# Hybrid decoder block: fewer expert pairs scattered, down projections moved behind the next gate and up, the router's end written out in order

## The chip, the cores and the metric

One core of a Trainium2 chip runs the whole program. The metric is the device time of one execution in microseconds. The kernel before took 1235.06 us (median of 3 runs, 1234.50 to 1239.01). Engines are called as in the profile: PE does matmuls (PEld loads its weights), DVE is the vector engine, ACT the scalar engine, POOL is GpSimd, SP only issues DMAs here. Sixteen DMA engines serve all queues.

## The reference

The block works on one sequence of 512 tokens with 1024 channels, all in float32. It has two parallel branches (a state-space scan and latent attention), a cross-attention to 256 memory rows, and a mixture of experts. The change touches the end of the cross-attention and the mixture, which is:

```
t = rms_norm(h, norm_moe)
g_logits = t @ w_rg + b_rg              # 4 groups
e_logits = t @ w_re + b_re              # 32 experts, 8 in each group
g_sel = argmax(g_logits);  g_w = softmax(g_logits)[g_sel]
top_v, top_i = top_k(e_logits of group g_sel, 2)
w_top = softmax(top_v) * g_w
h += sum over the 2 chosen experts e of
     w_top[e] * ((silu(t @ w_gate[e]) * (t @ w_up[e])) @ w_down[e])
return rms_norm(h, norm_final)
```

Each expert has gate and up weights of 1024 x 256 and down weights of 256 x 1024, 3 MB in float32, and 32 of them are read.

## The kernel before, in words

Everything up to the router has its order of instructions chosen by a planner, which works with a cost model of its own; from `chain` on (line 1111) the order on every engine and queue is the written one.

**Low parts.** Matmuls of the first stages split each weight into a high part (tile `WH`) and a low part. The low parts go in turn through three places: one in tile `WLa`, two in `WLb` (lines 134 to 152). When the stages are over, `YB` takes the place of `WLa`, and the one-hot matrices `OHt` take that of `WLb` (lines 1074 to 1076).

**Router.** `tok_proj` (line 857) adds the output of the cross-attention to `h`, 512 channels (`c`) and 128 tokens (`t`) at a time, and calls `router_tile(c, t)` for each. That squares `h` for the norm, transposes it on PE, copies the transposes to `tT` on ACT, and multiplies them by the router's weights (`logits`, 4 float32 matmuls of 36 columns, two instructions each). `keep_warm(n)` issues n transposes whose result nobody reads. Then DVE works through the routing in some 40 small steps: norm, logits, top group, top two experts, the place of each token within its expert (`ppos`, on PE), and `sl`, the slot number of each token's two choices.

**Slots.** Each expert has 64 slots, and a pair of experts `pr` 128 rows. Tokens past 64 in one expert go to a loop at the very end, which runs as often as needed. A one-hot matrix (tokens by slots) multiplied by token numbers and weights gives each slot's token: `onehots` builds it on DVE, 256 slots (a piece `c`, two pairs) at a time, and `places` reads out tokens, weights and scatter addresses with 8 matmuls and some 16 DVE steps of two or 16 columns. For pairs 0 and 1 `first_rows` reads only the token numbers, so that their gathers can start.

**A pair.** `fetch` or `first_rows` lets POOL gather the 128 rows of `h` from their copy `tD` in memory. `dispatch` transposes them (8 transposes) and scales them on DVE into `XG`. `gate_up` multiplies with both experts' weights, each on its 64 columns of the array (32 instructions), then asks SP for gate and up weights of pair `pr + 3`, whose tiles it has just freed. `hidden` makes silu(gate) * up on ACT and DVE, `turn` transposes that. `down` multiplies with the down weights (16 instructions). SP asks for the down weights of pair `pr + 3` behind `down_rows(pr)`; it has three places for them as well.

**Back to the tokens.** For pairs below `NS` = 11, `down_rows` weighs the result on ACT into `YB`, and POOL scatters the rows into a table `yD` in memory (one half for the first choice, one for the second). For the others `weigh` makes a high and a low part in `WHe` (ACT, then DVE), `ones_at` builds the one-hot matrix `oT` on DVE, and `combine` multiplies the two (16 matmuls, 8 DVE adds into `h`). The scattered rows come back as 16 table pieces `Yt` of 128 x 512 (lines 1387 to 1400): `left_rows` asks for two on POOL's queue, `add_left` adds two to `h` on DVE and asks for the next two. In pairs 12 to 15 that happens twice a pair: before `dispatch`, and behind `combine`.

**The loop** (lines 1405 to 1446) runs, for each pair: `gate_up`, `hidden`, from pair 12 on `add_left`, `dispatch` of the next pair, `places` or `onehots`, `fetch`, `down_rows` of the pair before, `turn`, and from pair 12 on `combine` of the pair before and `add_left`. Behind it `down_rows` and `combine` of pair 15 and the final norm follow, with the output in four DMAs.

Of the kernel before, what the change touches and what calls it, by code (L numbers as in the profile page):

```python
# [29 lines left out]
def block(tc, nc, I, out, dbg=None):  # L30
# [101 lines left out]
        return w  # L132

    WH = sb.tile([128, 3, 1024], F32R, name="WHt", tag="WH")
    WLa = sb.tile([128, 1, 1024], F32R, name="WLta", tag="WLa")
    WLb = sb.tile([128, 2, 1024], F32R, name="WLtb", tag="WLb")
    WL = (WLa[:, 0], WLb[:, 0], WLb[:, 1])
    nsp = [0]

    def wsplit(shape):  # L140
# [895 lines left out]
    def router_tile(c, t):  # L1036

        if t == 0:
            tT[c] = sb.tile([128, 4, S], F32, name=f"tT{c}", tag="wr", bufs=2)
            if not c:  # L1040
                plg.append(pB("plg"))
        jk = tmp([128, 512], BF, name="jk2")
        A.activation(jk, h[:, t, c * 512:(c + 1) * 512], AF.Square, scale=1.0 / 32, accum_out=sq2[:, c, t:t + 1])
        p = pB("ptt")
        for d in range(4):
            T.transpose(p[:, d * 128:(d + 1) * 128], h[:, t, c * 512 + d * 128:c * 512 + (d + 1) * 128], ident)
        o, v = tT[c][:, :, t * 128:(t + 1) * 128], p.rearrange("p (d t) -> p d t", d=4)
        A.activation(o, v, AF.Copy)
        if c:
            nc.scalar.dma_start(tD[t * 128:(t + 1) * 128], h[:, t])  # L1050
        if t > 1:
            logits(c, t - 2)
        if t == NT - 1:
            logits(c, t - 1)
            logits(c, t)
    tok_proj(I["w_xo"][0], tk(oxh, oxl), 1.0, router_tile, pB)
    keep_warm(45)
    if dbg:
        dbg("h2", h)
    rt = sb.tile([128, 512], F32, name="rt", tag="acT")  # L1060
# [10 lines left out]
    GRt = sb.tile([128, 3, D], F32, name="GRt", tag="WH")  # L1071
    GR = [GRt[:, i] for i in range(2)]
    XG = GRt[:, 2].rearrange("p (k n) -> p k n", k=KD)
    YB = sb.tile([128, D], F32, name="YB", tag="WLa")
    OHt = sb.tile([128, 2, NT, 256], F32R, name="OHt", tag="WLb")
    OHs = [OHt[:, i] for i in range(2)]
    NG4 = NT * 4
    gl, el = T4(rtile(NG4)), rtile(NT * 32)
    g1, jk1, jk2 = rtile(NT), rtile(NT), rtile(NG4)
# [19 lines left out]
        yield V.tensor_tensor(oh, rv, bcn(jk, n), op=OP.is_equal)  # L1099

    HG, HT, PI, W2 = {}, {}, {}, []
    def onehots(c, js=(0, 1), ts=range(NT)):

        n = slice(js[0] * 128, js[-1] * 128 + 128)
        s_ = slc[:, c - 1] if c else sl
        for t in ts:
            a = rt2[:, 256:512][:, n]
            V.tensor_scalar(a, iot1[:, n], s_[:, 0, t:t + 1], None, op0=OP.is_equal)
            stt(OHs[c % 2][:, t, n], iot1[:, n], s_[:, 1, t:t + 1], a, OP.is_equal, OP.add)

    chain = ExitStack()
    chain.enter_context(tc.manual_schedule())
# [34 lines left out]
    for s in range(2):  # L1147
        V.tensor_tensor(big2[:, s], EE[:, s], qs_, op=OP.mult)
    V.reduce_sum(sl, big2, axis=AX.X)
    onehots(0, (0,))  # L1150
    V.tensor_copy(qs_, pe_)
    V.tensor_tensor(slc.rearrange("p c s t -> p c (s t)"), sl.rearrange("p s t -> p (s t)")[:, None, :].to_broadcast([128, 7, 8]),
                    c256[:, :, None].to_broadcast([128, 7, 8]), op=OP.add)
# [86 lines left out]
    def places(c):  # L1240

        p = pA("pinf")
        for j in range(2):
            for t in range(NT):
                T.matmul(p[:, j * 8:j * 8 + 8], OHs[c % 2][:, t, j * 128:(j + 1) * 128], info[:, t],
                         start=t == 0, stop=t == NT - 1)
        pi = PI[c] = ov[:, 216 + c % 3 * 26:242 + c % 3 * 26]
        V.tensor_copy(pi[:, :16], p[:, :16])
        col = lambda i: pi[:, :16].rearrange("p (j x) -> p x j", x=8)[:, i]
        ix, sx = (ov[:, o + c % 3 * 2:o + 2 + c % 3 * 2].bitcast(I32) for o in (300, 306))  # L1250
        u, wa, w, hr, r = (pi[:, 16 + 2 * i:18 + 2 * i] for i in range(5))
# [64 lines left out]

    def weigh(p, n, hf, w):

        WHe, = W2
        yh, yl = (WHe[:n, i, hf * 512:(hf + 1) * 512] for i in range(2))  # L1320
        A.activation(yh, p[:n], AF.Copy, scale=w)
        stt(yl, p[:n], w, f(yh), OP.mult, OP.subtract)

    def combine(oT, n, after=None):

        WHe, = W2
        for t, hf in ((0, 0), (1, 0), (0, 1), (1, 1), (2, 0), (3, 0), (2, 1), (3, 1)):
            hs = slice(hf * 512, (hf + 1) * 512)
            p = pA("pcm")
            T.matmul(p, oT[:n, t * 128:(t + 1) * 128], WHe[:n, 0, hs], start=True, stop=False)  # L1330
            T.matmul(p, oT[:n, t * 128:(t + 1) * 128], WHe[:n, 1, hs], start=False, stop=True)
            V.tensor_add(h[:, t, hs], h[:, t, hs], p)
            if after and hf:
                after(t)
# [23 lines left out]
            nc.sync.dma_start(outr[:, t], fo[:, t])  # L1358

    first_rows(0)  # L1360
    onehots(0, (1,))
    first_rows(1)
    gfin = fo = None
    wcol = lambda pr: PI[pr // 2][:, 20 + pr % 2:21 + pr % 2]
    hcol_ = lambda pr: PI[pr // 2][:, 22 + pr % 2:23 + pr % 2]
    tcol = lambda pr: PI[pr // 2][:, pr % 2 * 8:pr % 2 * 8 + 1]

    def down_rows(pr):

        if pr >= NS:  # L1370
            for hf in range(2):
                weigh(down(pr, hf), 128, hf, wcol(pr))
        else:
            for hf in range(2):
                A.activation(YB[:, hf * 512:(hf + 1) * 512], down(pr, hf), AF.Copy, scale=wcol(pr))  # L1375
            sx = ov[:, 306 + pr // 2 % 3 * 2 + pr % 2:307 + pr // 2 % 3 * 2 + pr % 2].bitcast(I32)
            G.indirect_dma_start(out=yD, out_offset=bass.IndirectOffsetOnAxis(ap=sx, axis=0), in_=YB, in_offset=None,
                                 bounds_check=2 * S - 1, oob_is_err=False)
        if pr + 3 < NP:
            load_down(pr + 3)  # L1380

    def add_rows(pr, after=None):
        combine(ones_at(128, tcol(pr)), 128, after)

    Yt, ny = [], [0, 0]

# [12 lines left out]
            ny[1] += 1  # L1399
        left_rows(n)  # L1400

    keep_warm(22)
    dispatch(0)
    keep_warm(8)
    for pr in range(NP):
# [12 lines left out]
            continue  # L1418
        if pr == 1:
            turn(0)  # L1420
        if pr > NS:
            add_left(2)
        if pr + 1 < NP:
            dispatch(pr + 1)
        c = pr // 2 + 2
        if pr % 2 and c < NP // 2:
            places(c)
        elif c < NP // 2:
            onehots(c)
        if pr + 3 < NP:  # L1430
            fetch(pr + 3)
        down_rows(pr - 1)
        if pr == NS:
            Yt.append(sb.tile([128, 2, 512], F32, name="Yt", tag="WLa"))
            left_rows(2)
            W2.append(sb.tile([128, 2, D], F32R, name="WHe", tag="WLb"))
        turn(pr)
        if pr == 2:
            overflow()
        if pr > NS:  # L1440
            add_rows(pr - 1)
            add_left(2)
        if pr == NP - 2:
            fo = gslot(NP - 3, 0, [128, NT, D], "fo")
            gfin = gslot(NP - 3, 1, [128, D], "gfin")
# [105 lines left out]
```

## Time and profile before

| | us |
|---|---|
| median of 3 runs | 1235.06 |
| the profiled execution | 1232.03 |
| its span | 1229.9 |
| PE busy | 1157.7 (94%) |
| DVE busy | 709.1 (58%) |
| ACT busy | 497.2 (40%) |
| POOL busy | 98.8 (8%) |
| granted PE clock, mean | 0.976 |

All times in the rows below are microseconds from the span's start. Busy times are those of one execution; an engine that is busy is not one that sets the end. A line number is that of the kernel before, and where a helper issues the instruction, that of the helper: most three-operand DVE steps stand at line 55, and all warm-up transposes at line 77. A matmul's duration includes its way through the array, so durations of neighbours overlap. A granted clock of 1.00 is 2.4 GHz, of 0.50 is 1.2 GHz.

### The profile page before, as it was taken

The numbers are of one execution on the slowest core, as the hardware profiler recorded it, in microseconds if no ns is written. First come the engines' busy times: TensorE is split into PE (matmuls) and PEld (weight loads), VectorE is DVE, ScalarE is ACT, GpSimd is POOL, SyncE is SP. The second block draws the span as 40 slices with busy tenths as digits, with TensorE's granted clock in tenths as the row PEclk, the third lists the DMA queues.
The fourth block names the chain that finished last, engine by engine and source line by source line (L and its number), as shares of the span: only waits on it lengthen the run. The fifth ranks groups of instructions, "written<-read, shape, count | busy, mean of one in ns | idle before, by whom it ended". The sixth has DMA issues, their size and how long they took to land. (4 is left out here: it accounts for less than half of the span.)

```text
span 1229.9 us, 15623 instructions
## 1 busy us (share of the span) xinstructions
PE 1157.7 (94%) x5893; PEld 846.8 (69%) x5893; DVE 709.1 (58%) x1456; ACT 497.2 (40%) x941; POOL 98.8 (8%) x122
## 2 busy tenths in 40 slices
PE   8999999999999999999999999999998999786981
PEld 6787777777888888887777889888886343333441
DVE  4387878778762335547775738636326644223564
ACT  5445765866542223557774325535320111011012
POOL 0101102121000000101110000000000211011111
PEclk9999999999999999999999999999998999888996
DMA  3542432432322323311124364643725999999921
GB/s 113 157 120 62 146 94 95 133 110 69 103 88 83 103 88 128 88 46 50 56 86 172 121 221 131 196 159 123 288 85 227 410 420 419 419 419 420 413 111 70
DMA packets 104331, 210.43 MB, mean 171 GB/s; under 512 B 13624, under 2 KB 71765, under 8 KB 91966
## 3 DMA queue, kind: packets, MB, share of 16 engines
q1 hardware_dynamic: 96782, 193.11, 43.6%
q0 software_dynamic: 6896, 14.20, 3.5%
q10 hardware_dynamic: 576, 2.10, 0.4%
q8 instruction: 47, 0.77, 0.3%
q14 instruction: 30, 0.25, 0.1%
HBM read 199.33 MB, written 14.22 MB: 174 GB/s over the span
## 5 line engine op out<-in xcount | busy, mean ns | idle before, releaser
L151 ACT ACTIVATE WHt<-wr 128x1024 fp32r<-128x1024 f32 x125 | 132.2, 1059 | 266.5 <-PE pa L126 157.3
L152 DVE TENSOR_TENSOR WLtb<-wr,WHt 128x1024 fp32r<-128x1024 f32 x82 | 100.0, 1221 | 109.1 <-ACT WHt L151 56.8
L1287 PE MATMUL pgu<-gu,GRt 128*64 128x512 f32 x512 | 122.2, 617 | 11.1 <-DMA gu<-in_w_exp_up_dram 11.1
L126 PE MATMUL pa<-uh,WHt 128*128 128x512 f32 x488 | 128.0, 399 | 2.7 <-ACT WHt L151 2.7
L126 PE MATMUL pa<-ul,WHt 128*128 128x512 f32 x488 | 124.8, 393 | 0.0
L126 PEld LDWEIGHTS pa<-uh,WHt 128*128 128x128 f32 x488 | 89.8, 188 | 23.4 <-ACT WHt L151 3.1
L126 PEld LDWEIGHTS pa<-ul,WHt 128*128 128x128 f32 x488 | 90.5, 188 | 18.9 <-issue 0.7
L1287 PEld LDWEIGHTS pgu<-gu,GRt 128*64 128x64 f32 x512 | 39.6, 142 | 82.7 <-issue 77.5
L152 DVE TENSOR_TENSOR WLta<-wr,WHt 128x1024 fp32r<-128x1024 f32 x42 | 53.5, 1274 | 65.2 <-ACT WHt L151 41.4
L126 PE MATMUL pa<-uh,WLtb 128*128 128x512 f32 x320 | 82.6, 395 | 0.0
L55 DVE SCALAR_TENSOR_TENSOR ea<-ea,pgu 128x256 f32<-128x256 f32 x16 | 6.7, 420 | 110.6 <-ACT ea L1276 110.5
L1276 ACT ACTIVATE ea<-pgu,ov 128x256 f32<-128x256 f32 x16 | 7.6, 474 | 155.3 <-PE pgu L1287 144.1
L126 PEld LDWEIGHTS pa<-uh,WLtb 128*128 128x128 f32 x320 | 59.2, 188 | 13.0 <-issue 1.2
L713 DVE TENSOR_REDUCE sm<-psc 128x1 f32<-128x512 f32 (+2 forms) x64 | 30.4, 489 | 23.5 <-PE psc L711 20.3
L126 PE MATMUL pa<-uh,WLta 128*128 128x512 f32 x168 | 42.3, 391 | 0.0
L1307 PE MATMUL py<-dn,aT 128*64 128x512 f32 x176 | 40.2, 598 | 0.0
L1219 POOL DMA_INDIRECT GRt<-tD,ov x16 | 16.2, 1010 | 272.9 <-DMA dw<-in_w_exp_down_dram 144.9
L714 ACT ACTIVATE Pq<-psc,sm 128x512 f32<-128x512 f32 (+2 forms) x64 | 33.2, 528 | 10.6 <-DVE sm L713 10.1
L1330 PE MATMUL pcm<-WHe,oT 128*128 128x512 f32 x40 | 18.8, 470 | 18.8 <-DVE oT L1314 18.8
L126 PEld LDWEIGHTS pa<-uh,WLta 128*128 128x128 f32 x168 | 31.3, 188 | 6.4
L55 DVE SCALAR_TENSOR_TENSOR y<-pa,cols,y 128x509 f32<-128x509 f32 (+2 forms) x48 | 34.7, 743 | 1.6 <-ACT y L385 1.4
L1375 ACT ACTIVATE YB<-py,ov 128x512 f32<-128x512 f32 x22 | 15.1, 687 | 45.7 <-PE py L1307 42.7
(528 smaller groups left out, 2351.4 us busy)
## 6 DMA issues: line engine op xcount, KB each, us to landing
gu<-in_w_exp_gate_dram SPq DMA_DIRECT2D x32, 1024.0 KB, 20.8
gu<-in_w_exp_up_dram SPq DMA_DIRECT2D x32, 1024.0 KB, 21.4
wr<-in_w_in_dram SPq DMA_DIRECT2D x26, 1024.0 KB, 5.4
dn<-in_w_exp_down_dram SPq DMA_DIRECT2D x22, 1024.0 KB, 22.5
dw<-in_w_exp_down_dram SPq DMA_DIRECT2D x10, 1024.0 KB, 21.7
wr<-in_w_ssd_out_dram SPq DMA_DIRECT2D x8, 1024.0 KB, 4.9
wr<-in_w_xkv_dram SPq DMA_DIRECT2D x8, 1024.0 KB, 5.0
S6t<-ac_d SPq DMA_DIRECT2D x24, 256.0 KB, 4.2
```

The lines of the kernel that those rows point to most:

```text
L55: V.scalar_tensor_tensor(o, a, s, b, op0=op0, op1=op1, **k)
L126: T.matmul(o, a(k)[x], b(k)[y], start=first and n == 0, stop=last and n == 3 * nk - 1)
L151: A.activation(h, raw, AF.Copy)
L152: lo.tensor_tensor(l, raw, f(h), op=OP.subtract)
L713: V.reduce_max(mx, dst, axis=AX.X, negate=True)
L714: A.activation(P[:, ROFF[qc]:ROFF[qc] + n], dst, AF.Exp, bias=mx, accum_out=sm[:, 1, s, qc:qc + 1])
L1219: G.indirect_dma_start(out=GR[pr % 2], out_offset=None, in_=tD, in_offset=bass.IndirectOffsetOnAxis(ap=ix, axis=0), **k)
L1276: A.activation(a[:, :256], p[:n, :256], AF.Tanh, scale=hr)
L1287: T.matmul(p[s * 64:(s + 1) * 64].rearrange("p (j n) -> p j n", j=2), XG[:, k, s * 64:(s + 1) * 64], gu[s][:, :, k], start=k == 0, stop=k ...
L1307: T.matmul(p[s * 64:(s + 1) * 64], aT[:, k, s * 64:(s + 1) * 64], dn[s][:, k, hf * 512:(hf + 1) * 512], start=k == 0, stop=k == 1)
L1330: T.matmul(p, oT[:n, t * 128:(t + 1) * 128], WHe[:n, 0, hs], start=True, stop=False)
L1375: A.activation(YB[:, hf * 512:(hf + 1) * 512], down(pr, hf), AF.Copy, scale=wcol(pr))
```

## The change

- `WLa` and `WLb` become three tiles `WL0`, `WL1`, `WL2`. `YB` takes the place of the first, the two one-hot matrices that of the others. Piece 1 alone has its one-hots in the second, all other pieces in the first.
- `NS` goes from 11 to 7: pairs 7 to 15 go through `weigh` and `combine`. Their weighted rows stand in tiles that `rt` and `rt2` leave free, and in `WL2`.
- From pair 8 on `down_rows` of the pair before follows `gate_up` and `hidden` directly, ahead of `dispatch`. In it `oT` is built first, and kept for `combine`.
- Table pieces: the first two are asked at pair 7, and `add_left` stands once in each of pairs 8 to 15, behind `combine`. `onehots` stands behind that.
- From `router_tile(1, 0)` on PE runs in the written order. `logits` stands before or behind the transposes of the last tiles as the diff shows, and `keep_warm` has 34 transposes instead of 45, all behind the last logits.
- The one-hots of pairs 0 and 1 are built by three DVE operations over all four token tiles each, instead of eight over one tile each.
- `keep_warm` ahead of the first `dispatch` has 6 transposes instead of 22.

```
-    WLa = sb.tile([128, 1, 1024], F32R, name="WLta", tag="WLa")
-    WLb = sb.tile([128, 2, 1024], F32R, name="WLtb", tag="WLb")
-    WL = (WLa[:, 0], WLb[:, 0], WLb[:, 1])
+    WL = [sb.tile([128, 1024], F32R, name=f"WLt{i}", tag=f"WL{i}") for i in range(3)]
...
-    NP, NS = 16, 11
+    NP, NS = 16, 7
...
             if not c:
                 plg.append(pB("plg"))
+            else:
+                ending.enter_context(tc.manual_schedule(engines={mybir.EngineType.PE}))
+        if t == NT - 1:
+            logits(c, t - 2)
...
-        if t > 1:
+        if t == NT - 2:
             logits(c, t - 2)
         if t == NT - 1:
             logits(c, t - 1)
             logits(c, t)
+    ending = ExitStack()
     tok_proj(I["w_xo"][0], tk(oxh, oxl), 1.0, router_tile, pB)
-    keep_warm(45)
+    keep_warm(34)
+    ending.close()
...
+    def onehots(c):
+        for t in range(NT):
+            o = OHs[c == 1][:, t]
+            V.tensor_scalar(o, iot1[:, :256], slc[:, c - 1, 0, t:t + 1], None, op0=OP.is_equal)
+            stt(o, iot1[:, :256], slc[:, c - 1, 1, t:t + 1], f(o), OP.is_equal, OP.add)
+
+    def first_onehots(j):
+        it = iot1[:, None, j * 128:(j + 1) * 128].to_broadcast([128, NT, 128])
+        o2 = [tmp([128, 512], name="oa").rearrange("p (t n) -> p t n", t=NT) for _ in range(2)]
+        for s in range(2):
+            V.tensor_tensor(o2[s], it, bcn(sl[:, s], 128), op=OP.is_equal)
+        V.tensor_tensor(OHs[0][:, :, j * 128:(j + 1) * 128], o2[0], o2[1], op=OP.add)
...
         if pr >= NS:
+            oTs[pr] = ones_at(128, tcol(pr))
             for hf in range(2):
                 weigh(down(pr, hf), 128, hf, wcol(pr))
...
     def add_rows(pr, after=None):
-        combine(ones_at(128, tcol(pr)), 128, after)
+        combine(oTs.pop(pr), 128, after)
...
-    keep_warm(22)
+    keep_warm(6)
     dispatch(0)
...
-        if pr > NS:
-            add_left(2)
+        late = pr > NS
+        if late:
+            down_rows(pr - 1)
         if pr + 1 < NP:
             dispatch(pr + 1)
         c = pr // 2 + 2
         if pr % 2 and c < NP // 2:
             places(c)
-        elif c < NP // 2:
+        elif c < NP // 2 and not late:
             onehots(c)
         if pr + 3 < NP:
             fetch(pr + 3)
-        down_rows(pr - 1)
-        if pr == NS:
-            Yt.append(sb.tile([128, 2, 512], F32, name="Yt", tag="WLa"))
-            left_rows(2)
-            W2.append(sb.tile([128, 2, D], F32R, name="WHe", tag="WLb"))
+        if not late:
+            down_rows(pr - 1)
         turn(pr)
         if pr == 2:
             overflow()
-        if pr > NS:
+        if late:
             add_rows(pr - 1)
             add_left(2)
+            if pr % 2 == 0 and c < NP // 2:
+                onehots(c)
+        if pr == NS:
+            Yt.append(sb.tile([128, 2, 512], F32, name="Yt", tag="WL0"))
+            left_rows(2)
+            W2.append([sb.tile([128, 512], F32R, name=f"Wx{i}", tag=t) for i, t in enumerate(("acT", "selP"))])
+            W2.append([x[:, i * 512:(i + 1) * 512] for x in [sb.tile([128, 1024], F32R, name="Wy", tag="WL2")] for i in range(2)])
```

## Rows read from the trace of the kernel before

**Rows 1.** Busy time by stretch: stretch, length, each engine, PE clock, DMA share, GB/s.
```profile
930.00:960.00 30.00, 27.52 (x147) 18.41 (x147) 21.28 (x94) 0.89 (x3) 3.99 (x4) 0.84 0.57 221
...
1080.00:1110.00 30.00, 25.64 (x111) 11.50 (x112) 7.15 (x16) 3.37 (x7) 3.05 (x3) 0.89 1.01 419
...
1170.00:1200.00 30.00, 25.31 (x108) 12.00 (x106) 19.97 (x34) 4.46 (x8) 3.22 (x6) 0.94 0.26 96
```

**Rows 2.** Timeline, router's end, all engines: start, duration, instruction, [idle before <- releaser].
```profile
918.84 0.60 ACT L1048 ACTIVATE tT<-ptt 128x512 f32<-128x512 f32 x1 [0.52 <-PE ptt L1046]
...
920.73 2.38 PE L77 MATMUL pw<-ident 128*128 128x128 f32 x20
...
922.95 0.98 PE L1033 MATMUL plg<-MI,tT 128*128 128x36 f32 x8
...
923.97 0.31 DVE L1122 TENSOR_TENSOR rt<-plg,MI 128x144 f32<-128x144 f32 x1 [3.48 <-PE plg L1033]
...
931.04 0.29 DVE L1108 TENSOR_SCALAR rt<-MI 128x128 f32<-128x128 f32 x1
...
933.49 0.35 DVE L55 SCALAR_TENSOR_TENSOR OHt<-MI,rt 128x128 fp32r<-128x128 f32 x1
...
935.22 1.02 POOL L1219 DMA_INDIRECT GRt<-tD,ov  x1 [144.89 <-DMA dw<-in_w_exp_down_dram]
...
937.36 4.96 PE L77 MATMUL pw<-ident 128*128 128x128 f32 x22
```

**Rows 3.** The gathers of line 1219: from issue to landing.
```profile
DMA to landing us min/median/max: 4.8/8.3/9.7
```

**Rows 4.** Timeline of SP's queue: the last gate and up piece.
```profile
1143.75 0.33 SPq L977 DMA_DIRECT2D gu<-in_w_exp_up_dram  x1
```

**Rows 5.** The gate and up loads of line 977: from issue to landing.
```profile
DMA to landing us min/median/max: 6.9/21.4/24.3
```

**Rows 6.** DMA issues: table pieces, KB each, median us to landing.
```profile
Yt<-yD POOLq DMA_DIRECT2D x16, 256.0 KB, 6.5
```

**Rows 7.** Busy time by pair: pair 12, then pair 13.
```profile
1113.43:1142.06 28.63, 18.83 (x75) 9.58 (x74) 9.59 (x16) 2.89 (x6) 4.30 (x6) 0.82 1.02 418
1142.06:1160.36 18.30, 16.08 (x75) 7.26 (x75) 10.70 (x19) 2.12 (x4) 2.17 (x4) 1.00 1.01 414
```

**Rows 8.** Busy time while `places` runs: its matmuls, then its DVE steps.
```profile
1075.06:1076.10 1.04, 1.04 (x13) 1.02 (x13) 1.00 (x3) 0.00 (x0) 0.00 (x0) 1.00 1.04 433
1076.80:1079.50 2.70, 2.70 (x14) 0.72 (x10) 2.30 (x17) 0.69 (x1) 1.01 (x1) 1.00 1.01 422
```

**Rows 9.** Timeline of PE, expert pairs.
```profile
944.42 7.09 PE L1287 MATMUL pgu<-gu,GRt 128*64 128x512 f32 x32
...
1044.02 1.07 PE L1287 MATMUL pgu<-gu,GRt 128*64 128x512 f32 x2
1047.09 7.08 PE L1287 MATMUL pgu<-gu,GRt 128*64 128x512 f32 x30 [2.00 <-DMA gu<-in_w_exp_up_dram]
...
1065.00 9.22 PE L1287 MATMUL pgu<-gu,GRt 128*64 128x512 f32 x30 [4.79 <-DMA gu<-in_w_exp_up_dram]
...
1135.76 0.76 PE L1330 MATMUL pcm<-WHe,oT 128*128 128x512 f32 x1 [9.80 <-DVE oT L1314]
...
1156.41 0.47 PE L1330 MATMUL pcm<-WHe,oT 128*128 128x512 f32 x1 [2.22 <-DVE oT L1314]
...
1180.78 7.09 PE L1287 MATMUL pgu<-gu,GRt 128*64 128x512 f32 x32
...
1193.37 0.47 PE L1330 MATMUL pcm<-WHe,oT 128*128 128x512 f32 x1 [1.69 <-DVE oT L1314]
...
1203.01 0.47 PE L1330 MATMUL pcm<-WHe,oT 128*128 128x512 f32 x1 [2.06 <-DVE oT L1314]
```

**Rows 10.** Timeline of DVE: a table piece added in pair 12, combine's adds in pair 13.
```profile
1130.10 0.69 DVE L1398 TENSOR_TENSOR h<-h,Yt 128x512 f32<-128x512 f32 x1 [7.57 <-DMA Yt<-yD]
...
1157.15 4.87 DVE L1332 TENSOR_TENSOR h<-h,pcm 128x512 f32<-128x512 f32 x8 [0.89 <-PE pcm L1331]
```

More of the change, by code (lines that the diff above doesn't have):

```diff
@@ L1073, in block @@
     XG = GRt[:, 2].rearrange("p (k n) -> p k n", k=KD)
-    YB = sb.tile([128, D], F32, name="YB", tag="WLa")
-    OHt = sb.tile([128, 2, NT, 256], F32R, name="OHt", tag="WLb")
-    OHs = [OHt[:, i] for i in range(2)]
+    YB = sb.tile([128, D], F32, name="YB", tag="WL0")
+    OHs = [sb.tile([128, NT, 256], F32R, name=f"OH{i}", tag=f"WL{i + 1}") for i in range(2)]
     NG4 = NT * 4
@@ L1101, in block @@
     HG, HT, PI, W2 = {}, {}, {}, []
[L1102 to L1109, printed above, removed]
+    def onehots(c):
[9 more added lines that the diff above has]
+        V.tensor_tensor(OHs[0][:, :, j * 128:(j + 1) * 128], o2[0], o2[1], op=OP.add)
     chain = ExitStack()
@@ L1149, in block @@
     V.reduce_sum(sl, big2, axis=AX.X)
-    onehots(0, (0,))
+    first_onehots(0)
     V.tensor_copy(qs_, pe_)
@@ L1244, in places @@
             for t in range(NT):
-                T.matmul(p[:, j * 8:j * 8 + 8], OHs[c % 2][:, t, j * 128:(j + 1) * 128], info[:, t],
+                T.matmul(p[:, j * 8:j * 8 + 8], OHs[c == 1][:, t, j * 128:(j + 1) * 128], info[:, t],
                          start=t == 0, stop=t == NT - 1)
@@ L1317, in weigh @@
     def weigh(p, n, hf, w):
-        WHe, = W2
-        yh, yl = (WHe[:n, i, hf * 512:(hf + 1) * 512] for i in range(2))
+        yh, yl = (x[:n] for x in W2[hf])
         A.activation(yh, p[:n], AF.Copy, scale=w)
@@ L1324, in combine @@
     def combine(oT, n, after=None):
-        WHe, = W2
         for t, hf in ((0, 0), (1, 0), (0, 1), (1, 1), (2, 0), (3, 0), (2, 1), (3, 1)):
@@ L1329, in combine @@
             p = pA("pcm")
-            T.matmul(p, oT[:n, t * 128:(t + 1) * 128], WHe[:n, 0, hs], start=True, stop=False)
-            T.matmul(p, oT[:n, t * 128:(t + 1) * 128], WHe[:n, 1, hs], start=False, stop=True)
+            T.matmul(p, oT[:n, t * 128:(t + 1) * 128], W2[hf][0][:n], start=True, stop=False)
+            T.matmul(p, oT[:n, t * 128:(t + 1) * 128], W2[hf][1][:n], start=False, stop=True)
             V.tensor_add(h[:, t, hs], h[:, t, hs], p)
@@ L1360, in block @@
     first_rows(0)
-    onehots(0, (1,))
+    first_onehots(1)
     first_rows(1)
@@ L1366, in block @@
     tcol = lambda pr: PI[pr // 2][:, pr % 2 * 8:pr % 2 * 8 + 1]
+    oTs = {}
     def down_rows(pr):
         if pr >= NS:
+            oTs[pr] = ones_at(128, tcol(pr))
             for hf in range(2):
```

## The prediction

> **What bounds the kernel now.** I read the busy time by stretch first. Where the experts run, the 16 DMA engines are busy 1.01 of the time from pair 3 on, and they drop to 0.26 in the last full stretch [rows 1]. So the experts are bound by their weights until about 1170 us, and by what the engines still have to do after that. Then I read the timelines at both ends of that stream. Ahead of it stands the router: its last logits, a chain of small DVE steps, the first gather, and gate and up of pair 0. Only when that last one ends are pair 3's weights asked, so each us won there moves the whole stream. Behind it, gate and up of pair 15 start at 1180.78 [rows 9], some 15 us after their last piece can have landed: it was asked at 1143.75 and the median landing is 21.4 us, which gives 1165.2 [rows 4, 5]. So from pair 12 on PE lags behind the weights. Pair 12 took 28.63 us with 18.83 busy, pair 13 took 18.30 with 16.08 busy [rows 7]. The reason is seen in pair 12: DVE stood 7.57 us for a piece of the table [rows 10], and PE 9.80 us behind it, for the one-hot matrix `oT` [rows 9].
>
> Sums below are made against the profiled execution: span 1229.9 us, time 1232.03, which lies 3.0 below the median of 1235.06. The 3.0 is added back at the end.
>
> **Router's end.** Before, 20 warm-up transposes (2.38 us) run ahead of the last logits, which so start at 922.95, though their input was there at 919.44 (the ACT copy from 918.84, 0.60 us); DVE takes the logits up at 923.97 [rows 2]. Written out, the order has half a logits group more (0.5 us) ahead of the last transposes, so the copy behind them ends at 919.95; then follow the last group's 0.98 and some 0.3 of handing over. DVE starts at about 921.2: 2.8 us won. The bounds are 0 (other engines are still placed by the planner) and 3.5 (no wait at all behind the copy). The rn steps on DVE, which must be done too, end at 920.5 and hide. The 34 transposes left (0.119 us each, 4.0 us) end at 925.3, before the one-hot of the router is there, so they hold nobody up.
>
> **First one-hots.** Eight small DVE operations run from 931.04 to 933.84, 2.80 us [rows 2]. In their place come three of 128x512 with two tensors. The nearest row is the add of a table piece, 0.69 us [rows 10]: 2.0 us. The four matmuls behind them no longer run beside them, +0.4. Net 0.4 won, between -0.5 and +1.0. The gather, issued at 935.22 before [rows 2], is issued at about 932.0.
>
> **Gather and first pair.** A gather lands 4.8 to 9.7 us after its issue, median 8.3 [rows 3]. The first has the 4.8 of a queue running empty. Issued earlier, it falls among the weights of pair 2, so I take 6.5: landed at 938.5. Before, 22 transposes (937.36, 4.96 us) end just before 942 and dispatch follows, 2.5 us ahead of gate and up at 944.42 [rows 2, 9]. With 6 of them dispatch waits for the gather instead, from 938.5: gate and up at 941.0, 3.4 won. Against it stands the clock. Those 22 transposes take 0.225 us each and the 20 before took 0.119 [rows 2], so PE ran at 1.2 GHz here, and the granted clock over 930 to 960 is 0.84 [rows 1]. With less work ahead of it, gate and up of pair 0 can begin at 1.2 GHz. A gate and up that did after a wait took 9.22 us for 30 instructions, where 7.08 is the rule [rows 9]: 2.1 lost at that, I take 1.1. So the stream starts G = 2.3 us earlier, bounds -3.6 (all of pair 0 at half rate) and 4.5 (landing in 4.8, no clock lost).
>
> The Trainium skill (DMA: Bandwidth & Descriptors, section "Issuing engines are not separate DMA queues") says that DMAs from whatever engine run on the same 16 engines and interleave. By that alone the early gather would take the loaded 8.3 us and G would be 0.5, the sum 1219. The trace agrees in so far as that 8.3 is the median over all 16 gathers, most of them issued into the running stream [rows 3].
>
> **The stream.** Four scatters less: each moves at most 128 rows of 4 KB, half of them filled (1024 rows over 16 pairs of 128 places), so 4 x 0.26 = 1.05 MB less, 2.5 us at the 419 GB/s of the stream [rows 1]. Against that the table pieces of 256 KB [rows 6], of which pairs 11 to 13 asked the first 8 to 10, are now asked from pair 7 on, two a pair; some 6 more fall into the stream, 1.57 MB, 3.7 us. Net +1.2 us. The last gate and up piece can land at 1165.2 - 2.3 + 1.2 = 1164.1. SP's order of asking stays; it comes to the down weights a little earlier, and the queue is full anyhow.
>
> **Late pairs.** The weighted add ("combine": 16 matmuls and 8 DVE adds of together 4.87 us [rows 10]) now runs in pairs 8 to 15 and once behind, nine times and not five. One takes PE 3.95 us, from 1156.41 to the next pair at 1160.36 [rows 7, 9], so 15.8 us more. They lie where PE waited for weights: pairs 8 to 11 span 1046.0 to 1113.43 before, 67.4 us, for 4 x (16.08 - 3.95) + 2 x 1.0 = 50.5 us of work, which leaves 16.9 [rows 7 to 9]. What a pair costs I take from pair 13, which did all of it: 16.08 busy [rows 7]. Its idle 2.22 us was the wait for `oT` [rows 9], made last, behind both weighted halves. Now `oT` comes first and dispatch (eight transposes, 1 us at 0.119) lies between down and combine, so the wait goes; next late is DVE's second weighted half, about level with the turn's end. I take 16.3. Pairs 9 and 11 also carry `places`: 1.0 us of PE and 2.3 us of small DVE steps [rows 8] between dispatch and the adds, and the four PSUM tiles then make combine wait about 2: 19.1. One-hots of 3.5 us and the piece adds now stand behind the adds, and DVE is free again before the next hidden step. So from pair 8, whose weights let it run at 1046.0 before (1044.02 and a 2.00 wait [rows 9]), less G: 1043.7 + 5 x 16.3 + 2 x 19.1 = 1163.4 for gate and up of pair 15. That is level with the DMA bound of 1164.1. Two limits so close do not cover each other fully, so 1166: 14.8 us before 1180.78. Bounds: 1162 (G at 4.5, no coupling) and 1172 (each pair the 18.30 of pair 13).
>
> **Tail.** From there to the end everything stays but the two waits of 1.69 and 2.06 us for `oT` [rows 9], since `oT` now precedes the weighted halves. DVE still has to make the first half behind the earlier adds, so I take 3.2 of 3.75 (bounds 0 and 3.8).
>
> Other edits: three separate low-part tiles instead of one and two, the one-hot's temporary gone, one buffer instead of two for later one-hots. Each reader there ends a pair before the next writer, cover of over 10 us; without it up to 3 us. Zero.
>
> Sum: -14.8 - 3.2 = -18.0. 1232.03 - 18.0 + 3.0 = 1217.
>
> **Rivals.** (B) The combine goes on waiting for DVE, so that late pairs stay at pair 13's 18.30: 1043.7 + 7 x 18.3 = 1171.8, tail not shortened, gain 9.0: 1226. For it: DVE is busy 10.70 of pair 13's 18.30 us [rows 7], and more to do per pair now. Against: the order of `oT`. (E) The cold start: with 27 warm-ups fewer, all of gate and up of pair 0 runs at 1.2 GHz, G -3.6, 5.9 us later: 1223. For it: the clock was down there even with the 22 [rows 2]. Against: it had come back by 944.42, when pair 0 took 7.09 [rows 9]. The Trainium skill (TensorE: Matmul & The Clock Gate, section "Part 1") has the throttled state as the default that only activity lifts, which speaks for E; the row of 0.225 us agrees. (F) The fixed order does not bring the logits forward, 2.8 us lost: 1220. (D) Slower: the adds of table pieces, each pair now, block DVE as in pair 12. The hidden step, the turn, the release of weight slots and so the stream come late. It decides where late pairs average over (1180.78 + 3.2 - 1043.7) / 7 = 20.0 us. At 21.5, between pairs 13 and 12 (18.30, 28.63 [rows 7]), pair 15 starts at 1194.2: 13.4 - 3.2 = 10 us slower, 1245. Against: each piece is asked a pair ahead (16 us for a landing of 6.5 [rows 6]).
>
> **Numbers.** Forecast 1217 (1211 to 1220) 0.60; E 0.13; F 0.08; B 0.13; D 0.06. The range 1207 to 1228 takes in all but D and the edges. A measurement of this kernel tells 0.5%, 6 us: faster 0.89, within 0.05 (the slow edge of B), slower 0.06.
>
> **What would show it.** Router: DVE's first step on the logits at 921. Start: gate and up of pair 0 at about 941, and 7 to 8 us long. Late pairs: PE idle ahead of combine below 0.5 us, pair 12 near 16.3 and not 28.6. Pair 15's gate and up near 1166; combine of pair 15 without its 2 us wait. DMA share near 1.0 until about 1165. Wrong it is if late pairs average over 18.3, or if the stream starts after 951.5.

## The result, and the profile after

The changed kernel takes 1218.42 us (median of 4 runs, 1216.74 to 1221.47) against 1235.91 for the kernel before on the same chip (4 runs): a ratio of 0.986, 95% interval 0.983 to 0.989. That is 17.5 us faster. The forecast was 1217, so kind and size were right. The profiled execution took 1216.74 us with a span of 1215.0, which is 14.9 less than the span before, where the sum had -18.0.

The busy time by stretch, in the three stretches of [rows 1] (columns: stretch, length, PE, weight loads, DVE, ACT, POOL, PE clock, DMA share, GB/s):

```profile
930.00:960.00 30.00, 22.33 (x117) 12.64 (x117) 18.61 (x78) 0.90 (x3) 4.22 (x4) 0.83 0.58 237
...
1080.00:1110.00 30.00, 28.10 (x128) 11.20 (x127) 21.67 (x47) 2.92 (x6) 4.29 (x6) 1.00 1.01 416
...
1170.00:1200.00 30.00, 22.28 (x94) 9.31 (x90) 20.84 (x42) 9.20 (x16) 5.79 (x4) 0.91 0.17 67
```

In the middle stretch PE was busy 25.64 us at a clock of 0.89 before. Now it is busy 28.10 at full clock, and DVE 21.67 instead of 7.15, while the DMA share is 1.0 as it was. So the weighted adds did move into time in which PE had waited for weights. In the last stretch the stream is further gone, 0.17 instead of 0.26.

The same view by pair, from each gate and up to the next, pairs 8 to 13, answering to [rows 7]:

```profile
1046.34:1063.92 17.58, 17.39 (x75) 7.11 (x74) 7.13 (x13) 3.00 (x6) 3.22 (x4) 1.00 1.02 417
1063.92:1084.59 20.67, 18.05 (x84) 8.69 (x83) 15.30 (x42) 2.23 (x4) 2.15 (x3) 1.00 1.02 418
1084.59:1100.93 16.34, 16.32 (x76) 6.93 (x75) 10.01 (x18) 2.23 (x4) 2.15 (x3) 1.00 1.01 416
1100.93:1119.82 18.89, 17.00 (x83) 7.88 (x83) 15.27 (x42) 2.23 (x4) 2.14 (x3) 1.00 1.02 419
1119.82:1136.18 16.36, 16.32 (x75) 6.91 (x74) 10.01 (x18) 2.23 (x4) 2.14 (x3) 1.00 1.01 413
1136.18:1152.53 16.35, 16.32 (x76) 6.94 (x75) 10.02 (x18) 2.23 (x4) 1.10 (x2) 1.00 1.02 418
```

A late pair without table work takes 16.34 to 16.36 us with PE busy 16.32: PE hardly pauses. Pair 12 is one of them, 28.63 before. Of the 12.3 us that it gained, 9.8 were the wait for `oT`, and 2.5 mostly the clock: the same 75 matmuls were busy 18.83 us at a mean granted clock of 0.82 [rows 7], and take 16.32 at 1.00. Pairs 9 and 11, which carry `places`, have 2.6 and 1.9 us idle.

The timeline of PE over the expert pairs, answering to [rows 9] (start, length, line, instruction, count, in brackets the idle time before it and its releaser):

```profile
964.02 1.14 PE L1245 MATMUL pxg<-ident,GRt 128*128 128x128 f32 x8 [1.80 <-DMA GRt<-tD,ov]
...
965.87 5.35 PE L1316 MATMUL py<-dn,aT 128*64 128x512 f32 x16
...
1047.60 6.65 PE L1296 MATMUL pgu<-gu,GRt 128*64 128x512 f32 x29 [0.18 <-DMA gu<-in_w_exp_up_dram]
...
1054.09 0.59 PE L1296 MATMUL pgu<-gu,GRt 128*64 128x512 f32 x1
...
1059.18 0.48 PE L1337 MATMUL pcm<-Wx,oT 128*128 128x512 f32 x1
...
1065.74 6.62 PE L1296 MATMUL pgu<-gu,GRt 128*64 128x512 f32 x29 [0.74 <-DMA gu<-in_w_exp_up_dram]
...
1072.20 0.59 PE L1296 MATMUL pgu<-gu,GRt 128*64 128x512 f32 x1
...
1082.13 0.50 PE L1337 MATMUL pcm<-Wx,oT 128*128 128x512 f32 x1 [1.88 <-DVE h L1339]
...
1168.87 7.09 PE L1296 MATMUL pgu<-gu,GRt 128*64 128x512 f32 x32
...
1179.51 0.48 PE L1337 MATMUL pcm<-Wx,oT 128*128 128x512 f32 x1
...
1187.60 0.51 PE L1337 MATMUL pcm<-Wx,oT 128*128 128x512 f32 x1
```

Two things are to be seen. The combine (line 1337) starts without a wait for `oT` in pairs 8 and 15 and behind the last pair; the only wait left stands in the middle of a combine, at its ninth matmul, and is for DVE's adds: 1.88 us in pair 9 and 1.89 in pair 11. And the waits for weights of 2.00 and 4.79 us are down to 0.18 and 0.74. Those two cost more than they show, since PE has begun on the first weights meanwhile: gate and up starts at 1046.34 in pair 8 and ends, with the matmul of 1054.09, 8.34 us later, in pair 9 at 1063.92 and 8.87 us later, where 7.09 is the rule. So the weights still hold PE up by 1.25 and 1.78 us. The list of waits gives the idle time (engine, line, releaser: total us, times, longest):

```profile
PE pxg L1245 <- DMA GRt<-tD,ov: 5.6, 2, 3.8
...
PE pcm L1337 <- DVE h L1339: 3.8, 2, 1.9
...
PE pgu L1296 <- DMA gu<-in_w_exp_up_dram: 0.9, 2, 0.7
```

The same list of the kernel before has these two:

```profile
PE pcm L1330 <- DVE oT L1314: 18.8, 5, 9.8
...
PE pgu L1287 <- DMA gu<-in_w_exp_up_dram: 11.1, 3, 4.8
```

So 29.9 us of waiting in eight places became 4.7 in four, and 15.8 us of combines took part of the room. The router's end, the timeline of all engines, answering to [rows 2]:

```profile
913.44 0.69 DVE L55 SCALAR_TENSOR_TENSOR h<-pa,h 128x512 f32<-128x512 f32 x1 [10.56 <-PE pa L847]
...
920.91 1.93 PE L1031 MATMUL plg<-MI,tT 128*128 128x36 f32 x16
...
922.88 0.31 DVE L1131 TENSOR_TENSOR rt<-plg,MI 128x144 f32<-128x144 f32 x1 [0.58 <-PE plg L1031]
...
933.74 1.26 POOL L1228 DMA_INDIRECT GRt<-tD,ov  x1 [141.59 <-DVE ov L1236]
...
935.44 1.54 PE L77 MATMUL pw<-ident 128*128 128x128 f32 x6
...
940.77 1.97 PE L1245 MATMUL pxg<-ident,GRt 128*128 128x128 f32 x8 [3.79 <-DMA GRt<-tD,ov]
...
944.38 7.68 PE L1296 MATMUL pgu<-gu,GRt 128*64 128x512 f32 x32
```

Absolute times mislead here. The first row, where the last half of the output projection is first added to `h`, stood at 911.62 before: the whole program is 1.8 us late by then. That loss is some 800 us older. Busy time in one stretch near 97 us, first the kernel before, then the changed one:

```profile
95.70:99.10 3.40, 3.40 (x18) 2.79 (x18) 2.50 (x4) 1.63 (x2) 0.00 (x0) 1.00 0.00 0
```

```profile
95.70:99.10 3.40, 3.40 (x10) 2.65 (x9) 2.77 (x5) 0.04 (x1) 0.00 (x0) 0.50 0.00 0
```

For 3.4 us the granted clock is 0.50 and PE does 10 matmuls instead of 18. Another execution of the same changed kernel (the last experiment) has two such stretches, near 36 and 98 us, and is 3.7 us late at that row. The edits don't make them: e6 below, which has the same instructions up to that row, has none and is there at 911.62, and e2, which keeps the low-part tiles of before, has one and is there at 913.57. So I count from that row on. In the table h is the start of that add; the columns give us from h to DVE's first step on the logits, to the end of gate and up of pair 0, and to the start of gate and up of pair 15, and then from there to the end of the span.

| kernel | logits at DVE | end of gate/up 0 | gate/up 15 | rest |
|---|---|---|---|---|
| before | 12.35 | 39.89 | 269.2 | 49.1 |
| changed | 9.44 | 38.62 | 255.4 | 46.1 |
| predicted | 9.6 | 37.6 | 254.4 | 45.9 |

The predicted row is the prediction's 921.2, G = 2.3, 1166 and 3.2, less the 911.62 of before.

### The profile page after: what moved, and what is told of

The parts are those of the page before. It is cut to its first block, busy times and chain, and to the rows that moved or that the text cites. A ratio compares the mean times of both kernels' runs of the same rounds, so it can differ in the third digit from the quotient of the medians.

```text
span 1215.0 us, 15732 instructions
## 1 busy us (share of the span) xinstructions
PE 1165.5 (96%) x5930; PEld 846.5 (70%) x5930; DVE 732.1 (60%) x1490; ACT 498.0 (41%) x941; POOL 95.2 (8%) x118
## 5 line engine op out<-in xcount | busy, mean ns | idle before, releaser
L150 DVE TENSOR_TENSOR WLt<-wr,WHt 128x1024 fp32r<-128x1024 f32 x124 | 153.4, 1239 | 176.4 <-ACT WHt L149 99.0
L126 PE MATMUL pa<-uh,WLt 128*128 128x512 f32 x488 | 125.1, 394 | 0.0
L1296 PE MATMUL pgu<-gu,GRt 128*64 128x512 f32 x512 | 116.1, 598 | 0.9 <-DMA gu<-in_w_exp_up_dram 0.9
L126 PEld LDWEIGHTS pa<-uh,WLt 128*128 128x128 f32 x488 | 90.8, 188 | 19.6 <-issue 1.2
L1296 PEld LDWEIGHTS pgu<-gu,GRt 128*64 128x64 f32 x512 | 36.2, 138 | 70.6 <-issue 67.9
L1339 DVE TENSOR_TENSOR h<-h,pcm 128x512 f32<-128x512 f32 x72 | 43.8, 679 | 0.0
L126 PE MATMUL pa<-yl,WHt 128*128 128x512 f32 x128 | 32.8, 396 | 0.0
L126 PE MATMUL pa<-yh,WLt 128*128 128x512 f32 x128 | 32.3, 394 | 0.0
L126 PE MATMUL pa<-yh,WHt 128*128 128x512 f32 x128 | 32.2, 393 | 0.0
L459 ACT ACTIVATE dc<-S6t,ac 128x128 f32<-128x128 f32 x96 | 30.4, 388 | 0.8 <-POOL y L476 0.8
## 6 DMA issues: line engine op xcount, KB each, us to landing
gu<-in_w_exp_up_dram SPq DMA_DIRECT2D x32, 1024.0 KB, 21.7
dw<-in_w_exp_down_dram SPq DMA_DIRECT2D x10, 1024.0 KB, 21.2
```

The costliest lines, as they stand in the source:

```text
L126: T.matmul(o, a(k)[x], b(k)[y], start=first and n == 0, stop=last and n == 3 * nk - 1)
L150: lo.tensor_tensor(l, raw, f(h), op=OP.subtract)
L459: A.activation(dc[:, cs], R[:, cs], AF.Relu, scale=-1.0, bias=ac[:, c * 32 + h:c * 32 + h + 1])
L1296: T.matmul(p[s * 64:(s + 1) * 64].rearrange("p (j n) -> p j n", j=2), XG[:, k, s * 64:(s + 1) * 64], gu[s][:, :, k], start=k == 0, stop=k ...
```

## The experiments

Theory A, the prediction's: the late pairs bring nearly all of it, by two edits that need each other (fewer scatters, so that combines fill PE's idle time; `oT` first and down ahead of dispatch, so that they don't wait), and the router's end a little. Its rivals: the count of scatters alone does it; or the router's end does much of it, by starting the stream earlier.

**e1_late_only**: the changed kernel with the router's end, the first one-hots and the 45 and 22 warm-ups of before.

```
-            else:
-                ending.enter_context(tc.manual_schedule(engines={mybir.EngineType.PE}))
...
-    keep_warm(34)
-    ending.close()
+    keep_warm(45)
...
-        for s in range(2):
-            V.tensor_tensor(o2[s], it, bcn(sl[:, s], 128), op=OP.is_equal)
...
+        for t in range(NT):
...
-    keep_warm(6)
+    keep_warm(22)
```

> The late part of the change alone: 7 pairs scattered, down behind the next gate and up, oT first, table pieces a step ahead, three low-part tiles; the router's end, its warm-ups and the first one-hots are as before. Theory A (the gain is made in the late pairs and the tail, by waits that go): the stream starts as before at about 951.5, late pairs take 16.3 and twice 19, gate and up of pair 15 start at 1167 to 1170, the tail is 3 us shorter, gain 14 +- 2: 1220 to 1223. Theory B (the earlier start of the stream makes most of it): under 6 us gained, 1230 or more.

1219.92 us, ratio 0.988 (0.986 to 0.990). From h: logits at 12.34, gate/up 0 done at 39.9, as before; gate/up 15 at 258.0, rest 46.1. So the late part alone brings most of the gain, as A says: 14.1 us (1234.06 before on its chip) of 17.5. Its times overlap with those of the whole change, although its gate/up 15 stands 2.6 us later from h.

**e2_router_only**: the other half, the kernel before with the changed router's end, first one-hots and warm-ups.

> The other half alone: PE's written order at the router's end with 34 warm-ups, the first one-hots in three operations, 6 warm-ups ahead of the first dispatch; 11 pairs scattered and the loop as before. Theory A: logits some 2.9 us earlier, but the first gather lands under load and gate and up of pair 0 runs partly at 1.2 GHz, so that the stream starts only about 1 us earlier; the later pairs pass that on: gain 1 to 3, 1233 to 1235. Theory B: 8 us or more, 1228 or less.

1235.17 us, ratio 1.001 (0.999 to 1.002): nothing. From h, logits come at 9.9, 2.5 us earlier, and gate/up 0 ends at 38.9, 1.0 earlier. Gate/up 15 is at 269.5, as before. The 1.0 is gone by pair 2 already (58.5 from h, 57.6 before, since pair 1 takes 16.9 us instead of 15.0). Pairs 8 to 12 win 2.6, so that pair 13 begins 1.7 earlier from h than before, and it takes 21.1 us instead of 18.3. Its combine waits 3.68 us for `oT` and then runs at half clock for 3.4 us. So the router's end is not what does it. A had expected 1 to 3 us here: a miss in size, since the 1.0 us doesn't come through to the end.

**e3_ns11_new_order**: the changed order, but 11 pairs scattered.

```
-    NP, NS = 16, 7
+    NP, NS = 16, 11
...
         if late:
             down_rows(pr - 1)
+            add_left(2)
```

> The changed kernel with 11 pairs scattered again. Down still follows the next gate and up and oT stands first; with only four late pairs each has to add four table pieces, so two are added behind down and two behind combine. Theory A: PE waits for weights up to pair 12 (about 1113), the first piece's landing holds DVE once as before, some 7 us; the other waits go. Pair 15's gate and up at 1170 to 1175, gain 8 to 13, 1223 to 1228. Theory C (the count of scattered pairs is what matters, the order is worth nothing): as before the change, 1232 to 1236.

1223.98 us, ratio 0.992 (0.991 to 0.994), as A expected. In pair 12, DVE again stands for a table piece, and PE behind it; two rows of the timeline:

```profile
1130.24 0.69 DVE L1408 TENSOR_TENSOR h<-h,Yt 128x512 f32<-128x512 f32 x1 [3.42 <-DMA Yt<-yD]
...
1133.81 0.77 PE L1337 MATMUL pcm<-Wy,oT 128*128 128x512 f32 x1 [6.25 <-DVE GRt L1246]
```

Pair 12 takes 25.0 us, against 28.63 before and 16.36 in the changed kernel. With 11 scattered, the pieces of the table come only from pair 11 on, and the new order mends just part of that. Without the lower count, the order keeps 10.1 us of the gain.

**e4_old_order_ns7**: 7 scattered, but down where it was (behind dispatch, `places` and the fetch) and `oT` last, in the combine.

```
-            down_rows(pr - 1)            # ahead of dispatch
...
+        down_rows(pr - 1)                # ahead of turn
...
-        combine(oTs.pop(pr), 128, after)
+        combine(ones_at(128, tcol(pr)), 128, after)
```

> The changed kernel with the old order inside a late pair: down stands behind dispatch, places and fetch, oT is built last, ahead of combine. 7 pairs scattered and the table pieces as changed. Theory A: each late combine waits some 2.2 us for oT and the second weighted half, so pairs take about 18.3 and the two waits of the tail come back; pair 15's gate and up at about 1177, 1228 to 1232. Theory C: as the changed kernel, 1217 to 1221.

1229.67 us, ratio 0.996 (0.995 to 0.997). The combines wait again, 1.7 us each, and pairs take 17.8 to 19.3 us. Pairs 10, 12 and 14 take 19.3, where pair 13 takes 17.8: in them the granted clock is at 0.50 for 3.4 us behind the wait. Two of the waits:

```profile
1062.98 0.47 PE L1337 MATMUL pcm<-Wx,oT 128*128 128x512 f32 x1 [1.69 <-DVE oT L1323]
...
1082.05 0.47 PE L1337 MATMUL pcm<-Wx,oT 128*128 128x512 f32 x1 [1.72 <-DVE oT L1323]
```

So the count alone doesn't do it: without the order it keeps 4.4 us, less than a third of the gain. This is what the prediction's rival B describes. Each of the two edits is worth something alone (e3, e4), and neither brings all of it.

**e5_onehot_last**: the changed kernel with one instruction moved, `oT`, from ahead of the weighted halves into the combine.

```
-            oTs[pr] = ones_at(128, tcol(pr))
...
-        combine(oTs.pop(pr), 128, after)
+        combine(ones_at(128, tcol(pr)), 128, after)
```

In the changed kernel this instruction is the following one, in pair 8:

```profile
1056.14 0.45 DVE L1323 TENSOR_SCALAR oT<-MI,ov 128x512 fp32r<-128x512 f32 x1
```

> The changed kernel with one edit undone: oT is built ahead of combine again, behind the weighted halves and dispatch's steps on DVE; down still follows the next gate and up. It splits what the old order cost (1229.67 against 1218.42). Theory A (combine waits for what stands last on DVE, whatever PE does in between): oT comes 0.5 us behind dispatch's second step, combine starts some 2 us later, a pair takes about 17.9 and the two waits of the tail come back: 1228 to 1233, nearly all of it. Theory D (down's place ahead of dispatch is what counts, oT is hidden behind dispatch): 1218 to 1222.

1236.26 us, ratio 1.001 (1.000 to 1.002): the whole gain is gone, which is worse than A expected. Two combines, in pair 8 and in pair 9, and pair 9 by busy time:

```profile
1061.65 0.51 PE L1337 MATMUL pcm<-Wx,oT 128*128 128x512 f32 x1 [1.94 <-DVE oT L1323]
...
1083.44 0.77 PE L1337 MATMUL pcm<-Wx,oT 128*128 128x512 f32 x1 [3.66 <-DVE oT L1323]
```

```profile
1067.10:1090.00 22.90, 19.24 (x85) 10.28 (x84) 16.28 (x42) 2.23 (x4) 2.15 (x3) 0.85 1.02 418
```

DVE works through its instructions in the written order. With `oT` last, it stands behind dispatch's copies and, in pair 9, behind all the small steps of `places`, at 1082.81. PE waits 3.66 us, and the mean clock of that pair falls to 0.85 (0.50 for 6.8 us, from 1082.4). The pair takes 22.9 us instead of 20.67. The instruction itself is 0.45 us long in the changed kernel; its place is worth 17 us. A had only counted the waits, and not the clock behind them. It is also worse than e4, which has `oT` last and down in its old place: down ahead of dispatch pays only with `oT` first. `oT` first with down in its old place was not run, so what down's place adds to it is not shown.

**e6_places_behind**: the 1.9 us waits in pairs 9 and 11 come from `places` between dispatch and the adds. Here `places` and the fetch run behind the combine.

```
             add_rows(pr - 1)
+            if tab:
+                places(c)
+                fetch(pr + 3)
             add_left(2)
```

> The changed kernel with places and the gather that hangs on it moved behind combine in pairs 9 and 11, so that its small DVE steps no longer stand ahead of the adds. Theory A: the two PE waits of 1.88 us in combine go, PE could have pair 15's gate and up 3.8 earlier, but its weights land about 1167, so 1.5 to 2 come through: pair 15 at 1167 where it was 1168.9, 1215 to 1218. If PE alone were the bound: 3.8, 1213 to 1215. If places were hidden anyway: no change.

1214.57 us, ratio 0.985 (0.983 to 0.987). No combine waits, and pairs 9 and 11 take 19.20 and 17.85 us instead of 20.67 and 18.89 (the windows below leave out the first and last tenth of a us):

```profile
1061.92:1081.00 19.08, 18.16 (x83) 8.58 (x82) 13.92 (x27) 2.23 (x4) 1.11 (x2) 1.00 1.02 418
...
1097.40:1115.20 17.80, 17.79 (x83) 10.78 (x82) 13.98 (x27) 2.23 (x4) 1.11 (x2) 1.00 1.02 418
```

From h, gate/up 15 starts at 253.5 instead of 255.4: of the 3.8 us of waits, 1.9 come through, as A expected. Pair 15's last piece is asked at 1143.74 and lands 21.2 us later, at 1164.9, and PE starts gate and up 15 at 1165.12. So here the weights are the limit at pair 15. The times of the two kernels overlap within their intervals.

**e7_warm22**: the changed kernel with 22 warm-ups ahead of dispatch, not 6.

```
-    keep_warm(6)
+    keep_warm(22)
```

> The changed kernel with 22 warm-ups again ahead of the first dispatch, where the change has 6. If the few warm-ups are what lets pair 0 begin at 1.2 GHz: the 22 end about when the first gather lands (940.7), dispatch starts as now, and dispatch and gate and up of pair 0 end 1 to 2 us earlier, 951 or less from the same logits; in the total 0 to 2 us, 1216 to 1219. If the 22 stand in the way of the gathered rows, as before: pair 0 ends 1 us later. If neither, the same within 0.3 us.

1218.31 us, ratio 0.987 (0.985 to 0.989), the same time. But the start is different, and it splits what the start gained:

```profile
943.11 1.16 PE L1245 MATMUL pxg<-ident,GRt 128*128 128x128 f32 x8 [1.09 <-DMA GRt<-tD,ov]
...
945.08 7.09 PE L1296 MATMUL pgu<-gu,GRt 128*64 128x512 f32 x32
```

Dispatch waits for the gather here too and starts at 28.1 from h, 0.8 us later than with 6 warm-ups (27.3). But from there to gate/up 0 it takes 1.97 us and not 3.61, and gate/up 0 takes 7.09 and not 7.68: the granted clock is back at 1.00 from 941.4, ahead of dispatch, and in the changed kernel only from 945.7, 1.3 us into gate and up. It ends at 37.2 from h: 2.7 us earlier than before, and 1.4 earlier than in the changed kernel. So the router's end brought 2.7, and cutting the warm-ups gave 1.4 of it back.

**e11_all_three**: `places` behind; gate and up of pair 0 for one expert and then the other; and pair 2's gather issued early, ahead of dispatch 0 and not behind it, as the expectation had it. It overwrites the rows of pair 0, so dispatch 0 waits for that gather too, and pair 0 is computed from pair 2's rows: the output is wrong, and only the times of its parts are of use.

```
+        for k, s in ([(k, s) for s in range(2) for k in range(KD)] if pr == 0 else
+                     [(k, s) for k in range(KD) for s in range(2)]):
...
+    onehots(1)
+    first_rows(2)
```

> A try for a faster one: places behind combine; gate and up of pair 0 works through its first expert and then its second, so that the first one's weight tile is free 3.5 us earlier and the stream of weights starts earlier; the one-hots of pairs 2 and 3 are built while PE waits for the first gather, and the gather of pair 2 is issued right behind dispatch of pair 0, not behind the weights of the tokens. Theory A: the weights' bound of pair 15 moves from 1167 to 1163.5, PE's from 1168.9 by 3.8 (places) and by 1.8 to 3.5 (the wait for pair 2's rows and the half clock behind it) to about 1162 to 1163, together 1164: 4 to 5 us faster than the changed kernel, 1213 to 1215. If only one of the bounds moves, 1 to 2.

1224.87 us, ratio 0.993 (0.991 to 0.995): a miss by 10 us. The early gather holds PE up for 4.83 us ahead of dispatch, and gate/up 0 is far longer than in any other kernel:

```profile
945.93 1.97 PE L1246 MATMUL pxg<-ident,GRt 128*128 128x128 f32 x8 [4.83 <-DMA GRt<-tD,ov]
947.69 1.91 PE L77 MATMUL pw<-ident 128*128 128x128 f32 x8
949.53 12.41 PE L1297 MATMUL pgu<-gu,GRt 128*64 128x512 f32 x32
```

The granted clock over it is 0.99, so it isn't that. The 32 instructions are the same; only their order differs, and pairs 1 to 7 of this kernel, whose instructions go in turn, take 7.09. The two experts use different halves of the columns, and in turn they overlap.

**e12_early_gather**: the same idea, mended: rows of pairs 2 and 3 are worked out while PE waits for the first gather, and their gathers follow dispatch 0 and 1. `places` behind, gate/up in turn, 14 and 6 warm-ups.

```
-    keep_warm(6)
+    keep_warm(14)
+    onehots(1)
+    ix23 = [row_ix(2), row_ix(3)]
+    keep_warm(6)
     dispatch(0)
+    gather(2, ix23[0])
...
             dispatch(1)
+            gather(3, ix23[1])
```

> A second try for a faster one. Places behind combine, 20 warm-ups ahead of the first dispatch, and the token numbers of pairs 2 and 3 read early, while PE waits for the first gather, but each gather issued behind the dispatch that frees its rows. Gate and up of pair 0 goes through both experts together again. Theory A: from DVE's first step on the logits to the end of pair 0's gate and up 1 to 1.5 us less than in the changed kernel, pair 1 takes 13 to 14 us and not 16.8, and PE could have pair 15 at 1160, but its weights, which follow the start of the stream, land at about 1165: in all 2 to 5 us below the changed kernel, 1213 to 1216. If PE is the only bound, 8: 1210.

1214.06 us, ratio 0.984 (0.982 to 0.985). It has the lowest median here: each of its times (1214.01 to 1214.56) is under each of the changed kernel's on the same chip (e14, 1216.33 to 1220.02). The wait for pair 2's rows is gone:

```profile
942.79 1.16 PE L1249 MATMUL pxg<-ident,GRt 128*128 128x128 f32 x8 [0.30 <-DMA GRt<-tD,ov]
...
944.75 7.09 PE L1300 MATMUL pgu<-gu,GRt 128*64 128x512 f32 x32
...
961.84 1.04 PE L1249 MATMUL pxg<-ident,GRt 128*128 128x128 f32 x8
...
963.64 3.65 PE L1320 MATMUL py<-dn,aT 128*64 128x512 f32 x16
...
1046.94 8.24 PE L1300 MATMUL pgu<-gu,GRt 128*64 128x512 f32 x29 [3.29 <-DMA gu<-in_w_exp_up_dram]
```

From pair 1 to pair 2 it takes 13.0 us, where the changed kernel took 16.8 and e6 16.7, and pair 2 starts 5.2 us earlier from h than in e6 (52.5 for 57.7). Yet gate/up 15 starts only 2.5 us earlier (251.0 for 253.5). The last row says why: PE now reaches pair 8 ahead of its weights and waits 3.29 us. The stream takes back what PE wins.

**e13_places_warm22**: `places` behind and 22 warm-ups, without the early gathers.

> The changed kernel with places behind combine and 22 warm-ups ahead of the first dispatch, the rows of pairs 2 and 3 gathered as in the changed kernel. Theory A: stream 1.2 us earlier, the two 1.88 waits gone: 2 to 4.5 us below the changed kernel, 1214 to 1216. If the warm-ups are worth nothing: as with places alone, 1214.6 at its measurement.

1215.14 us, ratio 0.984 (0.983 to 0.986); gate/up 0 ends at 37.0 from h and gate/up 15 starts at 252.2. It lies between e6 and e12 by h; by time, the three can't be told apart with certainty.

**e14_after_again**: the changed kernel once more.

> The changed kernel once more, unchanged, beside the other two on the same chip: 1217 to 1220. Its profile tells how much of the 1.8 us by which all of its stages stood later from 97 us on belongs to the change: Theory A, none, it is a stretch at half clock early in the program that comes and goes between executions.

1219.28 us, ratio 0.987 (0.986 to 0.989). From h: 9.44, 38.8, 255.9, rest 46.1: within half a us of the other execution, though h itself is at 915.32. Between, it is 1.7 us ahead: pair 2 starts at 56.4 from h and not 58.1. It loses that in pair 8, where it waits 2.34 us for weights.

## Why the prediction was right

**The late pairs and `oT`: right, and the main term.** A plain late pair was put at 16.3 and takes 16.34 to 16.36. Pairs 9 and 11 were put at 19.1 and take 20.67 and 18.89; in pair 9 gate and up meets its weights as they land and lasts 8.87 us, 1.78 over the 7.09 of an undisturbed one. The wait of "about 2" for the four PSUM tiles (the accumulators that DVE's adds empty) is 1.88. Pair 8 takes 17.58, 1.3 more than put, and all of that is its gate and up, 8.34 long for the same reason. e4 and e5 show that the count alone does not make the 16.3 possible, and the order does; the prediction named the order as what speaks against B.

**Tail: right.** 3.2 predicted, 3.0 measured; the waits of 1.69 and 2.06 for `oT` are gone from the rows.

**Two limits level at pair 15: right, within 1.9 us.** The last gate and up piece and the landing of that line:

```profile
1145.27 0.33 SPq L975 DMA_DIRECT2D gu<-in_w_exp_up_dram  x1
...
DMA to landing us min/median/max: 6.9/21.7/24.0
```

This piece itself took 21.7 us, the median, so 1167.0 against PE's 1168.87. The prediction had 1164.1 and 1163.4, and 2.6 for the coupling. The two limits did meet, but earlier: at pair 15 PE had 1.9 us in hand, and in pairs 8 and 9 it lost 3.0 to the weights. That 2.6 is near this 3.0 is luck, since nothing in the working gives its size. e6 shows the limit of the weights itself: with PE faster, pair 15 starts 0.2 us behind the landing.

**G: the size was off.** Predicted 2.3, measured 1.27, counted from h. The steps up to the gather were right: logits 2.9 us earlier (2.8), first one-hots 0.4 (0.4). The gather lands 7.0 us after its issue, where I took 6.5. So dispatch starts 3.2 us earlier (27.3 from h for 30.5), near the 3.4 of the prediction. The term that was mis-sized is the clock: 1.1 was taken, and 1.9 it cost, 1.3 between dispatch and gate/up 0 (3.61 us for 2.31) and 0.6 in it (7.68 for 7.09). 3.2 - 1.9 = 1.3. And e7 shows that this was the price of the cut itself: with 22 warm-ups nothing of it is lost. (The upper bound of 4.5 was summed wrongly: a landing in 4.8 instead of 6.5 us adds 1.7 to the 3.4, which gives 5.1.) The Trainium skill (DMA: Bandwidth & Descriptors, section "Issuing engines are not separate DMA queues") had it that the gather shares the 16 engines with the weights; by that the prediction noted G = 0.5. The trace agrees as to the direction: 7.0 us beside 396 GB/s (933.7 to 940.8), 4.8 us beside 213 before (935.2 to 940.0).

**What a us at the start is worth: wrong as put.** "Each us won there moves the whole stream" holds for the asking of pair 3's weights only. e2 has 1.0 us at gate/up 0 and nothing at pair 15. By pair 2 the changed kernel has lost its 1.27 and 0.5 more (58.1 from h, 57.6 before): PE waits 1.80 us for pair 2's rows, as the kernel before did for 1.72, but behind it the clock is at 0.50 for 3.4 us in this execution, and down takes 5.35 us instead of 3.65.

**The sum.** Pair 15's gate and up was to start at 1166 and starts at 1168.87. Of these 2.9, 1.8 are the early half-clock stretch, 0.8 the late start of pair 8 (1044.5 without that stretch, 1043.7 predicted), and 2.8 the pairs 8 to 14 (122.5 for 119.7), less the 2.6 allowed for coupling. So 1166 came near by terms that were off in both directions, and the 1.4 us between 1217 and 1218.42 are closer than the working was. The rivals: B did not come, since combines don't wait for `oT`, and e4 shows what it would have been, E's cold start cost the 1.9 above and not a gate/up 0 wholly at half rate, F and D did not come (the logits came at 9.44 from h; late pairs average 17.5, not 21.5). Costs put at zero (separate low-part tiles, one buffer) show no new wait in the list of waits, and e6 reaches h at 911.62, as before.

## What to carry to other kernels

On an engine that works in order, put the small operand for which the next engine waits ahead of the large ones: 0.45 us of DVE work in the wrong place cost all of a 17 us gain. Before moving work into an engine's idle time, see whether its waits there come from the stream or from the order, since the count of scatters without the order kept less than a third, and the order without the count over half. Where two limits are level, a us won on one of them is worth less until the other moves too: e12 was 5.2 us ahead of e6 at pair 2 and 2.5 at pair 15.

## What the runs showed of the hardware

**Matmuls on two halves of the columns overlap if issued in turn.** 32 matmuls of 128*64 over 512 columns take 7.09 us in turn (e7, pair 0) and 12.41 us one half after the other (e11, pair 0), at a clock of 1.00 and 0.99. The Trainium skill (TensorEngine Tiling (Array Packing), section "Tiling Modes") says that different tiles can load weights and multiply in parallel; the two times agree with it, at 1.75 times.

**Half-clock stretches come and go between executions of the same kernel.** The changed kernel had one of 3.4 us by 100 us in one execution and two in another, 1.8 us of time each; behind the wait for pair 2's rows it had one in the first (pair 1 to 2 takes 16.8 us) and none in the second (14.9). A comparison by absolute times would have put these on the edits.

What makes one execution have them and another not stays open: no run here varied that alone.
